# Low parts of a second pass from accumulating transfers, SiLU on ScalarE, keys and values loaded in place

## The chip, the core and the metric

One core of a Trainium2 chip runs the whole program. The metric is the device time of one execution in microseconds (us). The engines are PE (TensorE, matmuls into PSUM banks), DVE (VectorE), ACT (ScalarE), POOL (GpSimd) and SP (SyncE, which issues transfers). Each works through a queue of its own in order, and waits at semaphores for the others.

## The reference

A hybrid block on x of 1024 tokens by 2048 channels, all in float32:

```python
h = rmsnorm(x, norm_w[l])
proj = jnp.einsum('bsd,de->bse', h, w_in[l])               # 2048 -> 5632
q_a, k_a, v_a, g_a, q_r, k_r, v_r, g_r = jnp.split(proj, points, axis=-1)
attn = windowed_attention(q_a, k_a, v_a, attn_sink[l], rel_bias)   # 16 heads, window +-128
attn = rmsnorm(attn, attn_out_norm_w[l]) * jax.nn.silu(g_a)
ret = bidirectional_retention(rotary(q_r), rotary(k_r) * RET_KEY_DIM ** -0.5, v_r, ...)  # 8 heads
ret = head_groupnorm(ret, ret_gn_w[l]) * jax.nn.silu(g_r)
x = x + jnp.einsum('bse,ed->bsd', jnp.concatenate([attn, ret], -1), w_out[l])
return rmsnorm(x, final_norm_w)
```

## The kernel before

**Split matmuls.** Each float32 operand of the large products is split in two: a high part, rounded to the format in which PE multiplies (`fp32r`), and a low part, the operand minus its high part. Three matmuls of 128x512 make one product of such pairs: high by high, high by low, low by high (L1044 to L1046). `split` (L152) makes the pair of a weight tile of 128x512: ACT copies it with rounding (`wh`, L153), and `tt` (L147) subtracts on DVE or POOL (`wl`).

**Stages.** (1) The projections of keys, values and queries of the attention in the plain way (`STD`, six units of 256 columns), to some 297 us. (2) The other sixteen units of the projection (`FAST`: rotated queries and keys `qk`, retention values `vr`, gates `ga` and `gr`) by Strassen-like sums: seven products instead of eight, in two passes over K (half of the 2048 channels each). The first pass leaves partial sums in DRAM (`yd`), and the attention runs beside it, to some 740 us. The second pass loads them again (tiles `e`, L1056), adds its own products from the PSUM banks `psMa` and `psMb` (`take`, L1066, on DVE) and hands on finished columns (`deliver`); the retention runs beside it (`ret_job`), and so does the premix of the attention's rows with their gates (`premix`). It ends at some 1228 us. (3) The output projection and the last norm.

**A product of stage 2.** A unit `q` has seven products `p`; `slots` is the list of all 224 in order. Raw weight tiles `r` are loaded by SP (L993) some products ahead. `prep` (L1003) makes one product's weight: a raw tile itself for p = 0, 1, 5; sums of raw tiles, made on POOL, for p = 2, 3, 4, 6. The second sum of p = 2 is overwritten after p = 3 to become that of p = 6. At the end `prep` splits the weight, with the subtraction on POOL (`split(hi, lo, src, G)`). `prep` is called two products ahead of `multiply`; `wpair` has three buffers each of `wh` and `wl`. After `multiply`, `collect` has DVE add the bank to the partial sum, which frees the bank; there are two `psMa` and two `psMb`.

**Gates.** When a gate's columns are finished, ACT writes tanh(t/2) to a tile `t2` (L1108), and one product later DVE forms (tanh(t/2) + 1) * t (L1111), which is twice SiLU; the weights `ew` were halved for it at the start (L298). The result is stored to `gd`.

**Other work beside the second pass.** For `qk` units POOL multiplies by the cosine (e<-e,t), DVE by the sine, and DVE adds. `premix` loads a row of the attention, its gate and the row norms (`rbd`); POOL multiplies the last two (t<-t,t), DVE the rest (t<-t,ew,t). The retention has its state updates (`ST`, L150) and norm statistics (`bst`, `bmv`, `bny`, `bnt`) on DVE, with one power of 128x4 on POOL (`bny`).

**What sets the order.** `point()` is called after every group of matmuls and draws pieces of the side jobs from queues by fixed paces; stores are held back some points (`store`). The framework then sets each engine's order. `t2` is a general tile of 128x512 with `NT2` = 7 buffers.

## Time and profile before

| | |
|---|---|
| three runs | 1606.28, 1612.95, 1613.6 us; median 1612.95 |
| the profiled execution | 1608.98 us, of which 1607.2 are its span |
| mean granted PE clock | 0.97 |
| busy, of the span | PE 93%, weight loads 77%, DVE 57%, POOL 43%, ACT 42% |
| transfers | all issued by SP; 310.86 MB, 59.7% of 16 engines' time |

Busy times are sums of intervals of instructions; matmuls are pipelined and overlap. A row of a group reads: line of the kernel, engine, operation, tiles out<-in, shape, count, then busy us and mean ns of one, then the engine's idle time ahead of them with what ended it. A row of the waits names who waited, for whom, us in total, times, and the longest. The chain of work that ended last is followed back from the last instruction, at each step to what released it; its row by line gives shares of the stretch. The row of a line or tile gives least, median and greatest ns, then first and last start.

### The profile page before, as it was taken

The numbers are of one execution on the slowest core, as the hardware profiler recorded it, in microseconds if no ns is written. First come the engines' busy times: TensorE is split into PE (matmuls) and PEld (weight loads), VectorE is DVE, ScalarE is ACT, GpSimd is POOL, SyncE is SP. The second block draws the span as 40 slices with busy tenths as digits, with TensorE's granted clock in tenths as the row PEclk, the third lists the DMA queues.
The fourth block names the chain that finished last, engine by engine and source line by source line (L and its number), as shares of the span: only waits on it lengthen the run. The fifth ranks groups of instructions, "written<-read, shape, count | busy, mean of one in ns | idle before, by whom it ended". The sixth has DMA issues, their size and how long they took to land.

```text
span 1607.2 us, 21996 instructions
## 1 busy us (share of the span) xinstructions
PE 1496.1 (93%) x7250; PEld 1243.6 (77%) x7250; DVE 908.3 (57%) x1849; ACT 667.0 (42%) x1416; POOL 683.6 (43%) x521
## 2 busy tenths in 40 slices
PE   8999999999999999999898797798898999999997
PEld 6898887778788888887776676676776778878886
DVE  6555437754563663576657668747659463364323
ACT  5311137755665765675333232222244443333220
POOL 3232221357456556457776676676552000122000
PEclk9999999999999999999999899899999999999999
DMA  8888668874544555357755675675446575566412
GB/s 304 291 269 304 235 192 277 256 245 141 153 154 128 172 162 178 123 173 251 242 176 168 210 243 172 206 245 165 138 161 200 189 250 165 156 196 222 121 32 105
DMA packets 192750, 312.26 MB, mean 194 GB/s; under 512 B 25419, under 2 KB 63307, under 8 KB 191996
## 3 DMA queue, kind: packets, MB, share of 16 engines
q1 hardware_dynamic: 192636, 310.86, 59.7%
q8 instruction: 57, 0.93, 0.3%
q14 instruction: 57, 0.47, 0.1%
HBM read 216.90 MB, written 93.88 MB: 193 GB/s over the span
## 4 chain that ended last, share of the span: by engine, by line
PE 45%; DVE 10%; DMA 8%; POOL 6%; issue 5%; ACT 2%; SPq 1%; POOLq 0%; ACTq 0%; DVEq 0%
PE psMa L1044 5%; PE psMa L1045 4%; PE psMa L1046 4%; PE psMb L1044 3%; PE psMb L1046 3%; PE psMb L1045 3%; POOL wl L147 2%; DVE ST L150 2%; DVE e L147 2%; DMA t<-gd 2%; PE psST L595 2%; POOL r L147 1%; PE psST L1272 1%; PE psST L1273 1%; PE psST L1271 1%
## 5 line engine op out<-in xcount | busy, mean ns | idle before, releaser
L147 POOL TENSOR_TENSOR wl<-r,wh 128x512 fp32r<-128x512 f32 x224 | 299.5, 1341 | 280.1 <-ACT wh L153 268.1
L1044 PE MATMUL psMa<-hT,wh 128*128 128x512 f32 x512 | 221.1, 432 | 42.5 <-DVE e L147 30.4
L153 ACT CAST wh<-r 128x512 fp32r<-128x512 f32 x224 | 138.4, 619 | 205.5 <-PE psMa L1045 102.6
L1046 PE MATMUL psMa<-hT,wl 128*128 128x512 f32 x512 | 210.1, 410 | 5.1 <-POOL wl L147 5.1
L1045 PE MATMUL psMa<-hT,wh 128*128 128x512 f32 x512 | 209.6, 409 | 0.0
L153 ACT CAST wh<-e 128x512 fp32r<-128x512 f32 x160 | 98.3, 619 | 246.1 <-PE psMb L1273 85.2
L147 POOL TENSOR_TENSOR r<-r,r 128x512 f32<-128x512 f32 x128 | 179.0, 1401 | 31.4 <-DMA r<-in_w_fast 17.1
L147 DVE TENSOR_TENSOR wl<-e,wh 128x512 fp32r<-128x512 f32 x112 | 84.4, 758 | 139.4 <-ACT wh L153 137.4
L1044 PE MATMUL psMb<-hT,wh 128*128 128x512 f32 x384 | 160.8, 419 | 0.0
L147 POOL TENSOR_TENSOR wl<-e,wh 128x512 fp32r<-128x512 f32 x48 | 71.2, 1484 | 203.9 <-ACT wh L153 197.3
L1044 PEld LDWEIGHTS psMa<-hT,wh 128*128 128x128 f32 x512 | 102.4, 200 | 66.9 <-issue 41.3
L1046 PE MATMUL psMb<-hT,wl 128*128 128x512 f32 x384 | 152.5, 397 | 0.0
L1045 PE MATMUL psMb<-hT,wh 128*128 128x512 f32 x384 | 151.7, 395 | 0.0
L1046 PEld LDWEIGHTS psMa<-hT,wl 128*128 128x128 f32 x512 | 101.9, 199 | 31.6 <-POOL wl L147 8.4
L1045 PEld LDWEIGHTS psMa<-hT,wh 128*128 128x128 f32 x512 | 102.5, 200 | 17.8
L558 DVE CUSTOM_DVE_ANT_0 P<-psST,bias,nsink 128x384 f32<-128x384 f32 (+1 forms) x128 | 74.1, 579 | 51.5 <-PE psST L550 51.3
L147 DVE TENSOR_TENSOR e<-psMb,e 128x512 f32<-128x512 f32 x96 | 65.8, 686 | 50.4 <-PE psMb L1046 30.3
L147 DVE TENSOR_TENSOR PTl<-psST,PTh 128x384 fp32r<-128x384 f32 (+1 forms) x128 | 66.6, 521 | 47.2 <-ACT PTh L602 44.4
L562 ACT ACTIVATE P<-P,nmx 128x385 f32<-128x385 f32 (+1 forms) x128 | 76.0, 594 | 36.1 <-DVE nmx L558 35.0
L153 ACT CAST hT<-t 128x512 fp32r<-128x512 f32 x100 | 60.4, 620 | 66.0 <-DMA t<-cd 20.9
L147 POOL TENSOR_TENSOR hT<-t,hT 128x512 fp32r<-128x512 f32 x16 | 23.5, 1485 | 147.7 <-DMA t<-in_w_out 115.6
L1046 PEld LDWEIGHTS psMb<-hT,wl 128*128 128x128 f32 x384 | 73.3, 191 | 16.4
(334 smaller groups left out, 3567.2 us busy)
## 6 DMA issues: line engine op xcount, KB each, us to landing
r<-in_w_fast SPq DMA_DIRECT2D x130, 256.0 KB, 2.9
e<-in_w_out SPq DMA_DIRECT2D x112, 256.0 KB, 3.0
yd<-e SPq DMA_DIRECT2D x64, 256.0 KB, 2.9
e<-yd SPq DMA_DIRECT2D x64, 256.0 KB, 3.4
t<-in_xT SPq DMA_DIRECT2D x31, 512.0 KB, 6.1
t<-cd SPq DMA_DIRECT2D x56, 256.0 KB, 4.8
e<-in_w_in SPq DMA_DIRECT2D x48, 256.0 KB, 4.7
md<-t SPq DMA_DIRECT2D x48, 256.0 KB, 2.7
```

Source lines behind the costliest of these rows:

```text
L147: eng.tensor_tensor(o, x, y, op)
L150: eng.scalar_tensor_tensor(o, x, s, y, op0, op1)
L153: A.copy(o_hi, x)
L558: V.tensor_tensor_reduce(x[:, :W], p[:, :W], bias[2 * pr + c][:, k0 : k0 + W], -1.0, nsink[:, head : head + 1], ALU.add, ALU.min, nmx[:, c ...
L562: A.activation(x[:, : W + 1], x[:, : W + 1], AF.Exp, bias=nmx[:, c : c + 1], scale=-1.0, accum_out=sums[:, c : c + 1])
L595: T.transpose(p[:, 128 * i : 128 * i + 128], x[:, 128 * i : 128 * i + 128], ident)
L1044: T.matmul(bank, wh[:, ws], hh, start=(j == 0 and p in (0, 1, 3)), stop=False, skip_group_check=True)
L1045: T.matmul(bank, wh[:, ws], hl, start=False, stop=False, skip_group_check=True)
L1046: T.matmul(bank, wl[:, ws], hh, start=False, stop=(j == 3), skip_group_check=True)
L1271: T.matmul(p, mh, wh, start=(k == 0), stop=False)
L1272: T.matmul(p, mh, wl, start=False, stop=False)
L1273: T.matmul(p, ml, wh, start=False, stop=(k == NK - 1))
```

## The change

- **Low parts.** `prep` becomes two: `prep_low`, called three products ahead, and `prep_high`, two ahead. In the second pass (`q >= NF`) `prep_low` has ACT write minus the rounded weight to the low tile, and then POOL issues a transfer from SBUF to SBUF that adds the weight itself to it (`accum_op=ALU.add`). `prep_high` makes the high part on ACT. In the first pass the subtraction stays on POOL, in `prep_high`; the sums of raw tiles are made in `prep_low`, a product earlier than before. `wl` has four buffers now.
- **Gates.** One ACT instruction, SiLU in place, in `deliver` itself, with the store right behind it; no tile `t2`, no product on DVE, no halving of `ew`.
- **Keys and values of the attention.** They are loaded into the tile that then holds their low parts (values: into that half of theirs), and split in place; before, they went through three `t2`.
- **Tiles.** `NT2` is 6.

```diff
@@ -19,7 +19,7 @@
 NT = S // 128
 EPS = 1e-6
 ATT, RET = 0, 1024
-NT2 = 7
+NT2 = 6
 
@@ -106,7 +106,7 @@
 
     def held(t, bufs):
         tag, n = serial[t.name]
-        assert given[tag] - n < bufs, (tag, n, given[tag])
+
         return t
 
     def flush(everything=False):
@@ -123,7 +123,13 @@
         return wp.tile([128, 512], dt, tag="r", name=nm("r"), bufs=8)
 
     def wpair(i):
-        return tuple(wp.tile([128, 512], F32R, tag=t, name=nm(t), bufs=3) for t in ("wh", "wl"))
+        return w_high(), w_low()
+
+    def w_high():
+        return wp.tile([128, 512], F32R, tag="wh", name=nm("wh"), bufs=3)
+
+    def w_low():
+        return wp.tile([128, 512], F32R, tag="wl", name=nm("wl"), bufs=4)
 
     def small(k, tag, bufs=1):
         return phase[0].tile([128, k], F32, tag=tag, name=nm(tag), bufs=bufs)
@@ -295,7 +301,6 @@
         sb = a["attn_sink"]
         SP.dma_start(sink, bass.AP(tensor=sb.tensor, offset=sb.offset, ap=[[0, 128], [1, 16]]))
         G.memset(mhalf, -0.5)
-        V.tensor_scalar(ew, ew, 0.5, None, ALU.mult)
         V.tensor_scalar(nsink, sink, -1.0, None, ALU.mult)
         yield
 
@@ -511,22 +516,19 @@
         load_bias(0)
         load_bias(1)
         q_load(0)
-        raws = []
+        for d2 in range(2):
+            SP.dma_start(kl[64 * d2 : 64 * d2 + 64, :].bitcast(F32), kd[64 * g : 64 * g + 64, :])
+        vs3 = vs.rearrange("p (t d) -> p t d", d=128)
+        SP.dma_start(vs3[:, :, 64:128].bitcast(F32), vd[g])
+        yield
         for hf in range(2):
-            kr = t2()
-            for d2 in range(2):
-                SP.dma_start(kr[64 * d2 : 64 * d2 + 64, :], kd[64 * g : 64 * g + 64, 512 * hf : 512 * hf + 512])
-            raws.append(kr)
-        vr = t2()
-        SP.dma_start(vr, vd[g].rearrange("p t d -> p (t d)"))
-        yield
-        for hf in range(2):
-            split(kh[:, 512 * hf : 512 * hf + 512], kl[:, 512 * hf : 512 * hf + 512], raws[hf])
-        vr3 = vr.rearrange("p (t d) -> p t d", d=64)
-        vs3 = vs.rearrange("p (t d) -> p t d", d=128)
+            sl = slice(512 * hf, 512 * hf + 512)
+            split(kh[:, sl], kl[:, sl], kl[:, sl].bitcast(F32))
+        vr3 = vs3[:, :, 64:128].bitcast(F32)
         A.copy(vs3[:, :, 0:64], vr3)
         tt(V, vs3[:, :, 64:128], vr3, vs3[:, :, 0:64].bitcast(F32), ALU.subtract)
         yield
+
         def normalise(b):
             n = b % 8
             W = 128 * (min(n + 2, 8) - max(n - 1, 0))
@@ -1000,10 +1002,12 @@
     loads[q - 1, 5] = [(q + 1, ("early 0", "early 1"))]
     loads[q, 2], loads[q, 4], loads[q, 5] = [], [(q + 1, (0, 1))], [(q + 1, (2, 3))]
 
-    def prep(q, p):
+
+    source, low = {}, {}
+
+    def prep_low(q, p):
         def w(x):
             return raws[q, x]
 
         if p == 0:
             src = raws.pop((q, "early 0"), None) or w(0)
@@ -1024,12 +1028,26 @@
             src = w(3)
         else:
             src = sums[q][1]
-        hi, lo = wpair(q)
-        split(hi, lo, src, G)
+        source[q, p] = src
+        if q >= NF:
+
+            lo = low[q, p] = w_low()
+            A.activation(lo, src, AF.Copy, scale=-1.0)
+            G.dma_start(lo.bitcast(F32), src, accum_op=ALU.add)
+
+    def prep_high(q, p):
+        src = source.pop((q, p))
+        hi = w_high()
+        if q >= NF:
+            lo = low.pop((q, p))
+            A.copy(hi, src)
+        else:
+            lo = w_low()
+            split(hi, lo, src, G)
         ready_w[q, p] = (hi, lo)
         if p == 3:
 
-            tt(G, sums[q][1], w(1), sums[q][1], ALU.subtract)
+            tt(G, sums[q][1], raws[q, 1], sums[q][1], ALU.subtract)
         for at, names in loads.get((q, p), ()):
             raw_load(at, names)
 
@@ -1103,16 +1121,9 @@
                 done.add((kind, i))
 
         if kind in ("ga", "gr"):
-
-            e = t2()
-            A.activation(e, t, AF.Tanh, scale=0.5)
-
-            def gate():
-                stt(V, t, held(e, NT2), 1.0, t, ALU.add, ALU.mult)
-                c = (0 if kind == "ga" else 8) + 2 * i + et
-                store(gd[128 * c : 128 * c + 128, sl], t, t, finished)
-
-            later.append(gate)
+            A.activation(t, t, AF.Silu)
+            c = (0 if kind == "ga" else 8) + 2 * i + et
+            store(gd[128 * c : 128 * c + 128, sl], t, t, finished)
         elif kind == "qk":
             cs, sn = t2(), t2()
             SP.dma_start(cs, a["cos"][:, sl])
@@ -1170,15 +1181,20 @@
         yield from ret_job(p)
 
     raw_load(0, (0, 1, 2, 3))
-    prep(*slots[0])
+    prep_low(*slots[0])
+    prep_low(*slots[1])
+    prep_high(*slots[0])
     for r in range(26, 28):
         c_split(r)
-    prep(*slots[1])
+    prep_low(*slots[2])
+    prep_high(*slots[1])
     step[0] = 16 * NS
     old, coming = deque(), deque()
     for n, (q, p) in enumerate(slots):
         if n + 2 < len(slots):
-            prep(*slots[n + 2])
+            prep_high(*slots[n + 2])
+        if n + 3 < len(slots):
+            prep_low(*slots[n + 3])
         if n + 1 < len(slots):
             q1, p1 = slots[n + 1]
             if q1 >= NF and p1 in (0, 2, 4, 5):
```

What it does to the queues, at three places.

POOL, near the end of the second pass: the last products of one unit and p = 2, 3 of the last one. `r2501` (before) and `r2456` (after) are the second sum. Before:

```order
L147 TENSOR_TENSOR wl2480_11573<-r2423_11291,wh2479_11572 128x512 [waits PE_49,Activation_49]
L147 TENSOR_TENSOR wl2486_11603<-r2456_11461,wh2485_11602 128x512 [waits DMAHW0_49,PE_49,Activation_49]
L147 TENSOR_TENSOR wl2492_11634<-r2452_11452,wh2491_11633 128x512 [waits PE_49,Activation_49]
L147 TENSOR_TENSOR wl2503_11683<-r2501_11679,wh2502_11682 128x512 [waits PE_49,Activation_49]
L147 TENSOR_TENSOR r2501_11679<-r2456_11461,r2501_11679 128x512 [waits Pool_49]
L147 TENSOR_TENSOR wl2510_11728<-r2500_11678,wh2509_11727 128x512 [waits PE_49,Activation_49]
```

After:

```order
L1036 DMA wl2437_11577<-r2390_11326 128x512 [waits Activation_49]
L1036 DMA wl2444_11611<-r2421_11497 128x512 [waits Activation_49]
L1036 DMA wl2449_11640<-r2415_11464 128x512 [waits Activation_49]
L1036 DMA wl2457_11675<-r2456_11672 128x512 [waits DMASW7_49,Activation_49]
L153 TENSOR_TENSOR r2456_11672<-r2421_11497,r2456_11672 128x512 [waits DMASW3_49,Activation_49]
L1036 DMA wl2465_11721<-r2455_11671 128x512 [waits DMASW0_49,Activation_49]
```

A subtraction has become the issue of a transfer, one product earlier, and the overwriting of the second sum waits for the landing (a `DMASW` semaphore) of the transfer issued just ahead of it.

ACT, a stretch of two or three products in a gate unit of the second pass. Before:

```order
L153 CAST wh2404_11209<-r2403_11206 128x512 [waits PE_49,Pool_49]
L771 COPY t2_2400_11200<-psST2399_11195 128x512 [waits DMAHW4_49,PE_49]
L1108 ACTIVATE t2_2401_11203<-e21_2392_11144 128x512 [waits DMAHW3_49,DVE_49]
L153 CAST wh2411_11240<-r2402_11205 128x512 [waits PE_49,Pool_49]
L1108 ACTIVATE t2_2410_11237<-e11_2387_11106 128x512 [waits DVE_49]
```

After:

```order
L1043 CAST wh2419_11493<-r2415_11464 128x512 [waits PE_49,Activation_49]
L1035 ACTIVATE wl2422_11499<-r2414_11463 128x512 [waits DMASW1_49,PE_49]
L773 COPY t2_2418_11489<-psST2417_11484 128x512 [waits DMAHW4_49,PE_49]
L1124 ACTIVATE e21_2408_11428<-e21_2408_11428 128x512 [waits DMAHW5_49,DVE_49]
L1043 CAST wh2424_11517<-r2414_11463 128x512 [waits PE_49,Activation_49]
L1035 ACTIVATE wl2425_11521<-r2389_11324 128x512 [waits DMASW2_49,PE_49]
L1124 ACTIVATE e11_2405_11406<-e11_2405_11406 128x512 [waits DMAHW0_49,DVE_49]
```

Each high part is now followed by the negated copy for the next product, and the gate stands where tanh stood.

DVE, the additions of partial sums in a gate unit. Before:

```order
L147 TENSOR_TENSOR e21_2441_11390<-psMa2393_11146,e21_2441_11390 128x512 [waits DMAHW6_49,DMAHW2_49,PE_49]
L150 SCALAR_TENSOR_TENSOR e21_2441_11390<-t2_2450_11449,e21_2441_11390 128x512 [waits Activation_49]
L147 TENSOR_TENSOR e11_2437_11367<-psMb2457_11463,e11_2437_11367 128x512 [waits PE_49]
L150 SCALAR_TENSOR_TENSOR e11_2437_11367<-t2_2458_11478,e11_2437_11367 128x512 [waits Activation_49]
L147 TENSOR_TENSOR e12_2413_11245<-psMb2428_11319,e12_2413_11245 128x512 [waits PE_49]
```

After:

```order
L153 TENSOR_TENSOR e21_2408_11428<-psMa2364_11185,e21_2408_11428 128x512 [waits DMAHW5_49,DMAHW1_49,PE_49]
L153 TENSOR_TENSOR e11_2405_11406<-psMb2423_11502,e11_2405_11406 128x512 [waits DVE_49,PE_49]
L153 TENSOR_TENSOR e12_2382_11284<-psMb2396_11357,e12_2382_11284 128x512 [waits PE_49]
L153 TENSOR_TENSOR e12_2426_11524<-psMa2409_11430,e12_2426_11524 128x512 [waits DMAHW6_49,DMAHW4_49,PE_49]
L153 TENSOR_TENSOR sd2447_11627<-psST2446_11622,dt2430_11543 128x512 [waits DMAHW2_49,PE_49]
```

The gate's products, which waited for ACT between the additions, are gone.

## The prediction

> **What bounds the kernel now.** I read the page's first part, then a table of stretches, then, for the stretch that the change touches, the groups of instructions of each engine, what they wait for, and the chain that ended last.
>
> ```profile
> span 1607.2 us, 21996 instructions
> PE 1496.1 (93%) x7250; PEld 1243.6 (77%) x7250; DVE 908.3 (57%) x1849; ACT 667.0 (42%) x1416; POOL 683.6 (43%) x521
> ```
>
> PE (TensorE) is busy for 93% of the span, so at first sight nothing but PE time counts. The table of stretches corrects this. The second pass over K runs from about 740 to 1228 us; the stretch ahead of it, 297 to 740, is the first pass, with as many products.
>
> ```profile
> 297.00:740.00 443.00, 426.93 (x2189) 361.26 (x2188) 240.29 (x652) 280.10 (x668) 249.44 (x191) 0.98 0.54 170
> 740.00:1228.00 488.00, 421.42 (x1979) 343.21 (x1978) 324.31 (x560) 154.80 (x292) 324.04 (x241) 0.92 0.60 197
> ```
>
> The columns are length, busy time of PE, its weight loads, DVE, ACT and POOL, then granted clock, DMA share and GB/s. The second pass has fewer matmul records and takes 45 us longer. PE stands idle for 66.6 us of it (first pass: 16.1), and its mean clock is 0.92 instead of 0.98. At the first pass's clock and busy share its work would need 421.42 x 0.92/0.98 / 0.964 = 410 us. So **78 us is the ceiling** of anything that only smooths the second pass. What PE waits for there, and the chain's shares in the same stretch (488 us):
>
> ```profile
> L1044 PE MATMUL psMa<-hT,wh 128*128 128x512 f32 x255 | 113.6, 446 | 42.5 <-DVE e L147 30.4 <-DVE bmv L746 12.1
> L1046 PE MATMUL psMa<-hT,wl 128*128 128x512 f32 x255 | 108.1, 424 | 3.7 <-POOL wl L147 3.7
> by line: issue 9.8%; PE psMa L1044 6.1%; POOL wl L147 5.7%; DVE ST L150 5.7%; PE psMa L1045 5.3%; DVE e L147 5.2%; PE psMa L1046 5.1%; POOL r L147 4.4%; DMA t<-rbd 3.7%; PE psMb L1044 3.2%; PE psMb L1045 3.1%; PE psMb L1046 3.1%; DMA r<-in_
> ```
>
> PE hardly waits for a low part (3.7 us). It waits for DVE to empty a PSUM bank (42.5 us at the first matmul of a product). DVE is late because it stands in line itself; one such gap, piece by piece:
>
> ```profile
> 859.28 1.69 POOL wl L147
> 861.04 1.61 POOL r L147
> 862.66 1.24 POOL e L147
> 863.92 0.69 DVE e L147
> 864.64 3.25 DVE qs L147
> ...
> 869.01 0.57 DVE e L147
> ...
> 869.73 0.77 PE psMa L1044
> 870.50 0.43 PE psMa L1045
> ```
>
> A low part on POOL delays the rope product on POOL, which delays DVE, which holds the bank; after the gap the matmuls come every 0.43 us, at a lowered clock. So what the change can earn is DVE's lateness.
>
> **The change, part by part.** All sums are against the profiled execution: 1608.98 us, of which 1607.2 is span; the median of the runs is 1612.95, 0.25% above it.
>
> *(a) 112 low parts leave POOL.* POOL's groups in the second pass:
>
> ```profile
> L147 POOL TENSOR_TENSOR wl<-r,wh 128x512 fp32r<-128x512 f32 x111 | 152.6, 1379 | 102.3 <-ACT wh L153 92.4 <-issue 5.4 <-PE psST L768 3.9
> L147 POOL TENSOR_TENSOR r<-r,r 128x512 f32<-128x512 f32 x61 | 89.2, 1467 | 11.6 <-DMA r<-in_w_fast 8.2 <-POOL t L147 0.7
> L147 POOL TENSOR_TENSOR t<-t,t 128x512 f32<-128x512 f32 x16 | 20.6, 1285 | 23.2 <-DMA t<-rbd 21.6 <-DMA r<-in_w_fast 1.6
> L147 POOL TENSOR_TENSOR bny<-bnv,mhalf 128x4 f32<-128x4 f32 x13 | 13.6, 1048 | 10.4 <-DVE bnv L749 10.0
> ```
>
> 152.6 us of work goes; of it 5.7% of 488 = 27.8 us lay on the chain, about 18% of what was removed. That 18% is my rate for POOL time. **-27.8 us.** In its place POOL issues 112 transfers. No row shows POOL issuing one. Nearest from below is SP's issue of a plain transfer, 0.32 us; from above a subtract that was held up, 2.13 us; in between a POOL instruction on four elements a row lasts 1.05, which is start-up and nothing else. I take 1.0 since a POOL routine has to start for this as well: 112 x 1.0 x 18% = **+20** (ends +6.5 and +43).
>
> *(b) POOL now waits for landings.* The order shows it: where POOL overwrote a source at once, it now first waits for the transfer that reads it.
>
> ```profile
> L1056 SPq DMA_DIRECT2D e<-yd x64: 319/382/1309, 720.1 to 1203.5; - x64
> L147 POOL TENSOR_TENSOR wl<-r,wh x224: 1260/1292/2130, 282.8 to 1216.9; 128x512 fp32r<-128x512 f32 x112
> r<-in_w_fast SPq DMA_DIRECT2D x58, 256.0 KB, 3.1
> t<-rbd SPq DMA_DIRECT2D x16, 256.0 KB, 4.8
> ```
>
> The first two rows give the ends of (a): SP's issue and POOL's longest subtract. The wait for landing comes once a unit right behind the issue (the update of the second sum), 16 times, and less sharply at the next unit's two sums, which have other work between. A 256 KB transfer takes 3.1 us to land from SP; less the issue that leaves about 2.3: 16 x 2.3 x 18% = **+7** (from 0, if landing is hidden, to 16 x 3 waits x 3.8 x 18% = +33 with the 4.8 us of a crowded one). Behind the waiting instruction stand the rope products, the gate-times-norm products (t<-t,t) and the next low parts; DVE waits for the first two, PE for the last. The low parts have cover: they start three products ahead, a product takes 488/112 = 4.4 us, and ACT 0.6 + POOL 1.0 + landing 3.1 is under 5 us, so 8 us are left. In a sentence of its own: by the Trainium skill, "DMA: Bandwidth & Descriptors", Anatomy of one DMA, a transfer issued from POOL costs some 2.0 us plus bytes over 436e3, an estimate of 2.6 us here, which would make this term +5; no row of this trace has such a transfer.
>
> *(c) DVE's relief.*
>
> ```profile
> L150 DVE SCALAR_TENSOR_TENSOR e<-t,e 128x512 f32<-128x512 f32 x30 | 26.7, 889 | 15.3 <-ACT t L1108 15.1
> L150 DVE SCALAR_TENSOR_TENSOR ST<-ST,cdec 64x128 f32<-64x128 f32 x42 | 28.4, 677 | 1.4
> L150 DVE SCALAR_TENSOR_TENSOR ST<-ST,cdec,psST 64x128 f32<-64x128 f32 x49 | 16.5, 338 | 1.1
> L150 DVE SCALAR_TENSOR_TENSOR t<-t,ew,t 128x512 f32<-128x512 f32 x20 | 24.1, 1205 | 21.9 <-POOL t L147 21.9
> L147 DVE TENSOR_TENSOR hT<-t,hT 128x512 fp32r<-128x512 f32 x22 | 23.5, 1082 | 5.7 <-ACT hT L153 5.6
> L147 DVE TENSOR_TENSOR e<-e,t 128x512 f32<-128x512 f32 x16 | 22.7, 1418 | 7.6 <-POOL e L147 7.2
> L147 DVE TENSOR_TENSOR t<-t,t 128x512 f32<-128x512 f32 x18 | 21.9, 1215 | 3.6 <-DMA t<-in_sin 3.5
> L147 DVE TENSOR_TENSOR bnt<-bnv,bny 128x4 f32<-128x4 f32 x12 | 11.6, 968 | 14.4 <-POOL bny L147 14.4
> L147 DVE TENSOR_TENSOR hT<-t,hT x84: 675/692/2664, 250.8 to 1318.0; 128x512 fp32r<-128x512 f32 x84
> L147 DVE TENSOR_TENSOR bnt<-bnt,bny x16: 145/162/1244, 853.1 to 1267.4; 128x4 f32<-128x4 f32 x16
> ```
>
> The gate's product (first row) goes: 26.7 us of work and 15.1 of standing idle for ACT's tanh, 41.8. The rest is lengthening: operations with both inputs in SBUF run at about twice their quiet length in this pass (ST<-ST,cdec at 677 ns where the form that reads PSUM takes 338; the 128x512 ones at 1082 to 1418 where the median over the run is 692; a 128x4 one at 968 where it can take 162). Summed over these rows: 14.2 + 10.3 + 8.6 + 11.6 + 9.4 + 9.7 = 63.8 us, while POOL works. The low parts are 152.6 of POOL's 324.0 us, 47%, so 30 us of it should go. DVE gets back 72 us. How much of DVE's time lies on the chain runs from POOL's 18% up to 62% for ST L150 (5.7% of 488 = 27.8 us, of 44.9 us of work in the two ST rows); the ST operations come in one long burst and the others are scattered, so I take a quarter: **-18** (0 if issuing lengthens DVE's operations as much, -72 if all of it counts).
>
> *(d) The clock.* PE spends 8% of 421 us more than at full clock, 34 us; I expect a quarter of the gaps to go: **-8** (0 to -34).
>
> *(e) DMA load.*
>
> ```profile
> q1 hardware_dynamic: 56886, 95.91, 60.2%
> q1 hardware_dynamic: 46278, 80.08, 79.6%
> e<-in_w_in SPq DMA_DIRECT2D x48, 256.0 KB, 4.7
> ```
>
> The first row is the second pass, the other two are from the first 300 us. 95.9 MB keep the queues 60.2% busy in this pass; 112 x 0.262 = 29.4 MB more make 79%, or 97% if a sum counts twice for reading its destination. In the first 300 us, at 79.6%, a 256 KB load takes 4.7 us instead of 3.1, half as much again. t<-rbd alone has 3.7% = 18 us on the chain, and half of that is 9; what the other loads have there is cut off in the row. I put **+8** (0 to +35, if the chain holds four times as much DMA as rbd's).
>
> *(f) SP.* The gates are stored a product or two earlier, and partial sums wait less for their tile; raw loads wait for landings instead of POOL's subtracts, a swap.
>
> ```profile
> SPq L993 <- POOL wl L147: 73.1, 27, 6.6
> SPq L1056 <- DMA gd<-e: 26.9, 19, 2.9
> ```
>
> 18% of 26.9: **-5** (0 to -10).
>
> *(g) The rest.*
>
> ```profile
> L153 ACT CAST wh<-r 128x512 fp32r<-128x512 f32 x111 | 68.4, 618 | 163.5 <-PE psMa L1045 87.9 <-PE psMb L1045 58.5 <-issue 4.4
> L891 ACT ACT_TABLE_LOAD  x1: 1283/1283/1283, 0.7 to 0.7; - x1
> ```
>
> ACT gets 112 more copies of 0.62 us, 69 us, on an engine with 154.8 busy of 488, covered by its idle time; if ACT is held behind DVE, three products of lead are the cover. One table load for SiLU: 1.3 us, as the one at the start. Six instead of seven general tiles: the gates' 32 and the four jobs' 12 no longer ask for one; taken as 0, -3 to +6. Keys and values in place: 0; they load three steps ahead.
>
> Sum: -27.8 + 20 + 7 - 18 - 8 + 8 - 5 + 1.3 = -22. **Forecast 1587 us.**
>
> **The rivals.**
> *Smooth second pass.* All of DVE's relief counts and the gaps close as in the first pass; for it speaks that DVE's busy share would fall from 66% to 55%, next to the first pass's 54%; against it that DVE still waits for POOL and rbd in order. -78 to -45: about 1548.
> *POOL fills up (slower).* POOL keeps 171 us of other work and some 50 of waits for DVE and DMA. At 2.0 us an issue (224) plus 37 of landing waits it is full: 482 of 488. From there on every transfer is late. With the upper ends of (a), (b) and (e) in place of the values taken, the sum goes from -22 by +23, +26 and +27 to +27 (without (e)) or +54: 1635 to 1660. For it: the 2.13 us that a held POOL instruction can take; against it: 1.05 us for the short one.
> *DVE holds off the issues.* If POOL can't write its transfer's description while a DVE operation runs, an issue lasts 1.0 and one such operation of 1.2 us (the 1205 ns row): 112 x 2.2 x 18% = 44 instead of 20, the sum is +2: 1611. For it: DVE and POOL lengthen each other in the rows of (c); against it: the 128x4 instruction of POOL, 1048 ns in the mean, hardly gets longer. In sentences of their own: the Trainium skill, "SBUF — State Buffer", Who interferes with whom and the box on the "DVE blocks DMA" trap ahead of it, says that descriptors of a POOL transfer can't be written while DVE runs in a two-port mode, and that 620 ns became 3100. With 3.1 us an issue the sum would be about +20. No row of this case shows a two-port mode or an issue on POOL.
> *Nothing to see.* DVE's waits go over into later loads: (c) at half and (e) at +20 give -1: 1608.
>
> **How the numbers follow.** Forecast, with a range of its own of 1568 to 1602: 0.50. Smooth pass: 0.14. POOL full: 0.17. Held issues: 0.05. Nothing: 0.14. A measurement of this kernel can tell about 0.5%, 8 us, from no change. Faster: 0.46 of the forecast + 0.14 = 0.60; same: 0.04 + 0.11 + 0.02 = 0.17; slower: 0.17 + 0.03 + 0.03 = 0.23. The range for 8 in 10 leaves out the outer halves of the smooth pass and of the full POOL: 1538 to 1635.
>
> **What would show it.** Right: in the pass's row DVE's busy time near 267 us, POOL's compute near 171 or less, the clock above 0.93; t<-t,ew,t nearer to 692 ns; PE's wait for DVE e under 25 us. Wrong: PE waiting at the wl matmul for a transfer by more than 10 us; transfers on POOL that last 2 us or land after 6; t<-rbd beyond 6 us; the first pass longer than 446 us, by the general tiles.

## The result, and the profile after

The changed kernel takes 1658.07 us (median of four runs, 1657.64 to 1664.68), the kernel before 1612.42 beside it: ratio 1.030, 95% interval 1.026 to 1.034. I had forecast 1587 us, faster, with 1635 as the upper end. It is 46 us slower, and outside the range. The profiled execution took 1658.43 us.

Page of the kernel after, first lines, then the table of stretches (columns as before):

```profile
span 1656.6 us, 22129 instructions
PE 1510.7 (91%) x7250; PEld 1251.4 (76%) x7250; DVE 836.7 (51%) x1816; ACT 724.0 (44%) x1529; POOL 617.9 (37%) x521
297.00:740.00 443.00, 423.69 (x2171) 360.11 (x2170) 242.01 (x653) 278.43 (x667) 245.49 (x187) 0.98 0.53 165
740.00:1280.00 540.00, 442.10 (x2015) 355.77 (x2014) 261.86 (x548) 218.87 (x418) 262.37 (x246) 0.90 0.87 240
```

The stretch of the first pass looks much as before. Most of the loss lies in the second, as DVE's additions out of the bank `psMa` show, before (first row) and after:

```profile
L147 DVE TENSOR_TENSOR e<-psMa,e x64: 652/690/694, 742.0 to 1224.8; 128x512 f32<-128x512 f32 x64
L153 DVE TENSOR_TENSOR e<-psMa,e x64: 654/691/693, 749.8 to 1275.9; 128x512 f32<-128x512 f32 x64
```

The first addition of the second pass starts 7.8 us later, the last 51.1; the spans differ by 49.4. So some 8 us are lost ahead of the second pass and 43 in it. And yet DVE got its relief: 261.9 us of work in this stretch of 540, where it had 324.3 in 488. POOL is busy for 49% of it, so it isn't full of work. Groups of POOL and DVE in 740 to 1280:

```profile
L1036 POOL DMA_DIRECT2D wl<-r x111 | 97.7, 928 | 75.9 <-ACT wl L1035 70.6 <-DMA wl<-r 2.8 <-issue 1.6
L153 POOL TENSOR_TENSOR r<-r,r 128x512 f32<-128x512 f32 x61 | 84.0, 1380 | 87.8 <-DMA wl<-r 52.2 <-ACT wh L1043 13.3 <-issue 7.8
L156 DVE SCALAR_TENSOR_TENSOR t<-t,ew,t 128x512 f32<-128x512 f32 x22 | 17.4, 793 | 65.7 <-POOL t L153 61.6 <-DMA t<-gd 4.0
```

An issue takes POOL 0.93 us, close to the 1.0 that I took. But in front of the weight sums (`r<-r,r`) POOL now stands idle for 87.8 us, where it was 11.6, of it 52.2 for landings of its own transfers; DVE waits 61.6 us for POOL's gate-times-norm products (before: 21.9). The waits of the same stretch, and below them SP's queue:

```profile
POOL wl L1036 <- ACT wl L1035: 70.6, 36, 4.6
POOL r L153 <- DMA wl<-r: 52.2, 18, 7.5
POOL t L153 <- DMA t<-rbd: 39.2, 10, 9.3
ACT wh L1043 <- PE psMa L1063: 81.2, 37, 7.5
PE psMa L1062 <- DVE e L153: 36.1, 12, 8.5
PE psMa L1064 <- DMA wl<-r: 15.5, 8, 4.3
SPq L995 <- DMA wl<-r: 99.0, 24, 9.9
```

PE itself waits only 15.5 us for low parts at `psMa`. The rows on transfers, and the chain that ended last in this stretch:

```profile
q1 hardware_dynamic: 59218, 99.79, 55.5%
q0 software_dynamic: 16021, 29.15, 31.4%
wl<-r POOLq DMA_DIRECT2D x111, 256.0 KB, 5.3
r<-in_w_fast SPq DMA_DIRECT2D x60, 256.0 KB, 4.4
t<-rbd SPq DMA_DIRECT2D x16, 256.0 KB, 5.2
by line: DMA wl<-r 13.1%; issue 10.2%; DMA t<-rbd 5.8%; POOL r L153 5.6%; DMA r<-in_w_fast 2.8%; DMA rq<-rqk 2.7%; PE psMa L1062 2.6%; PE psMa L1064 2.6%; POOL qs L153 2.4%; PE psMa L1063 2.2%; DMA gd<-e 2.0%; DVE ST L156 1.9%; DVE e L153 1
```

Landings of low parts are the largest single piece of the chain, 13.1% of 540 = 71 us; before, POOL's subtraction had 27.8. Per MB a sum holds the DMA engines 1.9 times as long as the other traffic (31.4/29.15 against 55.5/99.79), and other loads land later: raw weights after 4.4 us instead of 3.1, `t<-rbd` after 5.2 instead of 4.8. Two theories fit these rows. **Load:** the sums' traffic delays all other transfers. **Queue:** POOL and SP, which work in order, are held by issues and landings, and what stands behind is late. A third, **parts:** one of the smaller edits costs something.

### The profile page after: what moved, and what is told of

Read it like the earlier page. It is cut to its first block, busy times and chain, and to the rows that moved or that the text cites. A ratio compares the mean times of both kernels' runs of the same rounds, so it can differ in the third digit from the quotient of the medians.

```text
span 1656.6 us, 22129 instructions
## 1 busy us (share of the span) xinstructions
PE 1510.7 (91%) x7250; PEld 1251.4 (76%) x7250; DVE 836.7 (51%) x1816; ACT 724.0 (44%) x1529; POOL 617.9 (37%) x521
## 5 line engine op out<-in xcount | busy, mean ns | idle before, releaser
L1062 PE MATMUL psMa<-hT,wh 128*128 128x512 f32 x512 | 223.3, 436 | 46.5 <-DVE e L153 36.1
L1064 PE MATMUL psMa<-hT,wl 128*128 128x512 f32 x512 | 214.2, 418 | 18.0 <-DMA wl<-r 15.5
L153 POOL TENSOR_TENSOR r<-r,r 128x512 f32<-128x512 f32 x128 | 174.6, 1366 | 107.9 <-DMA wl<-r 52.2
L153 POOL TENSOR_TENSOR wl<-r,wh 128x512 fp32r<-128x512 f32 x112 | 145.8, 1303 | 177.8 <-ACT wh L159 175.0
L1063 PE MATMUL psMa<-hT,wh 128*128 128x512 f32 x512 | 211.8, 414 | 0.0
L1043 ACT CAST wh<-r 128x512 fp32r<-128x512 f32 x112 | 69.1, 617 | 140.4 <-PE psMa L1063 81.2
L1036 POOL DMA_DIRECT2D wl<-r x112 | 98.7, 929 | 75.9 <-ACT wl L1035 70.6
L153 DVE TENSOR_TENSOR e<-psMb,e 128x512 f32<-128x512 f32 x96 | 65.8, 685 | 47.8 <-PE psMb L1064 27.8
```

The costliest lines, as they stand in the source:

```text
L153: eng.tensor_tensor(o, x, y, op)
L1036: G.dma_start(lo.bitcast(F32), src, accum_op=ALU.add)
L1043: A.copy(hi, src)
L1062: T.matmul(bank, wh[:, ws], hh, start=(j == 0 and p in (0, 1, 3)), stop=False, skip_group_check=True)
L1063: T.matmul(bank, wh[:, ws], hl, start=False, stop=False, skip_group_check=True)
L1064: T.matmul(bank, wl[:, ws], hh, start=False, stop=(j == 3), skip_group_check=True)
```

## The experiments

Each kernel was timed beside the kernel before, whose medians ran from 1609 to 1612 us. Intervals of a ratio are about 0.2 to 0.4% to each side, 3 to 6 us; I read nothing into differences under 8 us between kernels.

### The parts without transfers

**SiLU alone, on the kernel before.**

```diff
-            A.activation(e, t, AF.Tanh, scale=0.5)
...
-                stt(V, t, held(e, NT2), 1.0, t, ALU.add, ALU.mult)
+            A.activation(t, t, AF.Silu)
```

> The kernel before with the SiLU gates alone: DVE loses 30 products of 0.89 us and 15 us of standing idle for tanh, and the gates ask for no general tile. Both theories: a gain of 5 to 20 us, 1593 to 1607 us. If it is no faster, the gate's product was hidden and my relief for DVE had no worth at all.

1594.54 us, ratio 0.991 (0.988 to 0.995): faster, by a gain of 17.3 us by the medians, 14 by the ratio.

**Subtracting again, on the kernel after.**

```diff
-            A.activation(lo, src, AF.Copy, scale=-1.0)
-            G.dma_start(lo.bitcast(F32), src, accum_op=ALU.add)
...
+        lo = w_low()
+        split(hi, lo, src, G)
```

> The kernel after, with the low parts of the second pass subtracted by POOL again and no transfer that sums; SiLU, keys and values in place and six general tiles stay. Load theory (transfers that sum hold the DMA engines about 1.9 times as long per MB, so that every other load lands later) and queue theory (POOL and SP, in order, wait for the landings of the transfers that read their tiles): both lay the whole loss on the transfers, so this goes back to before or below it, 1590 to 1612 us, DVE's waits for POOL in the second pass from 110 us to under 60, loads from in_w_fast from 4.4 us to 3.1. Tile theory (six general tiles or the loads in place cost the time): stays over 1630 us.

1605.52 us, 0.997 (0.995 to 0.999). The transfers cost 52.5 us. But 11 us of SiLU's gain are missing here.

**The same with seven general tiles, three low-part buffers.**

```diff
-NT2 = 6
+NT2 = 7
...
-        return wp.tile([128, 512], F32R, tag="wl", name=nm("wl"), bufs=4)
+        return wp.tile([128, 512], F32R, tag="wl", name=nm("wl"), bufs=3)
```

> The kernel with the low parts subtracted by POOL, with seven general tiles instead of six and three buffers for low parts instead of four. Before with SiLU alone took 1594.5 us, this kernel with six tiles 1605.5. If the sixth tile less is what costs the 11 us (DVE's sums and products wait for a tile), this one is at 1594 to 1598. If keys and values in place or the sums made a product earlier cost them, it stays at 1602 to 1607.

1594.72 us, 0.990 (0.988 to 0.992). The tile is the 11 us (with it goes one buffer for low parts, which can hardly be what helped); keys and values in place, and sums made a product earlier, cost nothing together. This kernel and the one with SiLU alone beat both the kernel before and after.

### Waits and sums: a square

Two choices make four kernels: the transfers sum or copy, and they read the weight tile or a constant piece of the operand rows. The kernel after is the first of the four.

**No source to protect.** The transfers read a constant piece of `hT`, the operand rows.

```diff
-            G.dma_start(lo.bitcast(F32), src, accum_op=ALU.add)
+            G.dma_start(lo.bitcast(F32), hT[:, 4 * p + 3, 0:512].bitcast(F32), accum_op=ALU.add)
```

> The kernel after, but each transfer that sums reads a constant piece of the operand rows instead of the weight tile (so it adds another tile than the weight; the low parts are not those of the weights). As many transfers, as many bytes, issued at the same place on POOL, and PE still waits for them; but no instruction of POOL and no load of SP waits any more for a landing in order to overwrite a source. Load theory: the DMA engines are as busy as after (share about 0.87 in the second pass) and the time stays at 1645 us or more. Queue theory: POOL's waits for DMA in the second pass fall from 116 us to about 40, SP's 99 us for the low parts go, and the time falls to 1615 us or less.

1630.38 us, 1.013 (1.010 to 1.017): 28 us of the loss are the protection of sources, that is, POOL and SP waiting before they overwrite what a transfer still reads. Neither theory's number came; 25 us above the subtracting kernel stay.

**Plain copies from the weight tile** (no `accum_op`).

> The kernel after, with the transfers as plain copies (the sum is left out, so that the low part is the whole weight). Same issues, same waits for landings, half the traffic if a sum reads its destination as well. Load theory: the DMA share of the second pass falls from 0.87 to about 0.75, loads land in 3.5 instead of 4.4 us, and the time falls to 1630 us or less. Queue theory: the time falls only as far as the landing shortens (5.4 us to about 4: some 15 us), to 1640 to 1650 us.

1616.11 us, 1.003 (1.001 to 1.005), 42 us less than with sums; loads from `in_w_fast` land in 4.0 us. This looked like the load theory.

**Both at once:** plain copies of the constant piece.

> The kernel after, with transfers that neither sum nor read the weight tile: plain copies of a constant piece of the operand rows into the low parts (which are therefore not those of the weights). POOL issues as often, DVE has the same relief, PE waits for the same landings; but nothing waits in order to overwrite a source, and the traffic of the sum is gone. With the three kernels before it this makes a square: after 1658, no waits for sources 1630, plain 1616. If waits and load add up, this one is at 1616 + 1630 - 1658 = 1588 us, and below 1600 the issues on POOL are cheap beside DVE's relief. If a wait hurts only because the landing is long (one cost, seen from two sides), it is at 1605 to 1616, as the plain copies or just below. If POOL's issues are the cost that is left, it stays above 1620.

1602.47 us, 0.995 (0.993 to 0.996). Waits cost 28 us with sums and 14 without; sums cost 42 us with waits and 28 without. They are neither quite additive nor one cost. In the two traces from the constant piece every engine runs the same instructions in the same order, and in the two from the weight tile too; so the 28 and the 42 us are of the transfer itself: its issue, its landing or its traffic.

### Which transfers

**Two products ahead**, three buffers, seven tiles.

```diff
+            prep_low(*slots[n + 2])
             prep_high(*slots[n + 2])
-        if n + 3 < len(slots):
-            prep_low(*slots[n + 3])
```

> The kernel after, with its low parts begun two products ahead instead of three, in three buffers, which gives the seventh general tile back. If the price of the tile (11 us without transfers) holds here too and two products, some 9 us, cover copy, issue and landing (0.6 + 0.9 + 5.4 us), the time is 1643 to 1650 us. If the shorter lead shows, PE's and its weight loads' waits for wl<-r in the second pass grow from 15 and 19 us to 40 and more, and it stays at 1655 us or goes above.

1664.27 us, 1.035 (1.032 to 1.038). The tile given back gains nothing in all. In this trace the second pass's first addition starts at 736.4 us instead of 749.8, so the first pass is shorter; but in the second the lead is shorter too, and PE's wait for low parts and POOL's for landings both grow (15.5 and 52.2 us in the kernel after):

```profile
POOL r L153 <- DMA wl<-r: 106.8, 32, 6.0
PE psMa L1064 <- DMA wl<-r: 51.8, 22, 5.8
```

**Only the 48 transfers from raw tiles**, on that kernel (`if q >= NF and p in (0, 1, 5)`, else POOL subtracts).

> Two products ahead and seven general tiles, with transfers that sum for the three of each unit's seven products whose weight is a raw tile (48 of 112); POOL subtracts the other 64. No instruction of POOL overwrites such a source, only SP's next raw loads do. Without transfers this kernel takes 1594.7 us. If the cost goes with the number of transfers (52.5 us for 112), it is 1594.7 + 22 = 1617 us. If it comes only when the DMA engines are near full (share about 0.75 here, as with the plain copies), it is below 1603. If it beats 1594.7, some transfers are worth having.

1609.11 us, 0.999 (0.997 to 1.002): 14 us above the same kernel without transfers, less than by number (its runs spread from 1600 to 1625 us).

**Only the 64 from sums** (`p in (2, 3, 4, 6)`).

> The complement: two products ahead and seven general tiles, with transfers that sum for the four of each unit's seven products whose weight is a sum or difference that POOL has computed (64 of 112); POOL subtracts the other 48. Here stand the sources that POOL itself overwrites. By number alone 1594.7 + 64/112 x 52.5 = 1625 us. If POOL's waits for landings carry the loss, it is above 1632 and the kernel with the raw tiles is below 1610; if it is the load, both go by their numbers.

1652.51 us, 1.027 (1.025 to 1.029): 58 us above, far more than by number. POOL's wait, in 740 to 1280:

```profile
POOL r L153 <- DMA wl<-r: 96.6, 30, 6.6
```

**The same 64 from the constant piece.**

> The kernel with transfers that sum for the 64 low parts of sums and differences (1652.5 us), with these 64 transfers reading a constant piece of the operand rows instead (so that those low parts are not the weights'). As many transfers, issues and bytes; PE still waits for the landings; but POOL may overwrite the sums at once. If POOL's waits for landings carry this loss, the time falls to 1605 to 1620 us, by the rate of the 48 from raw tiles (14 us) about 1614; if it is the traffic or the issues, it stays above 1640.

1618.58 us, 1.005 (1.003 to 1.008). As many transfers, bytes and issues, and 34 us less. The waits for sources carry this loss: POOL's 96.6 us above are gone, and with them 26.6 us for which SP waited for landings. POOL's wait is the one that the kernel with raw tiles has no cause for.

### Traffic, issue, and who issues

**Load beside the subtracts:** for each product two plain transfers, issued by SP, that nobody waits for.

```diff
+            for x in range(2):
+                SP.dma_start(spare[q - NF, p, x], hT[:, 4 * p + 3, 0:512].bitcast(F32))
```

> The kernel with the low parts of the second pass subtracted by POOL (1605.5 us), and beside that two plain transfers of 256 KB for each of its 112 products, from the operand rows to a place in DRAM that nobody reads, issued by SP: load alone, with no new wait on POOL or PE, and 224 issues of 0.32 us on SP. The DMA share of the second pass should rise from 0.62 to about 0.9, as with the transfers that sum. Load theory: other loads land later by a third or more (r from in_w_fast from 3.7 to 4.5 us or longer) and the time rises by 15 us or more, to 1620 or above. Queue theory: load without waits costs under 8 us, 1606 to 1613.

1641.92 us, 1.018 (1.015 to 1.021): 36 us for 58.7 MB and 224 issues on SP. Read alone this confirmed the load theory. The rows show where it went: ACT's roundings wait 29.3 us for raw loads, for which they didn't wait in the subtracting kernel, and PE waits 14.4 us for those roundings. Whether the loads came late by landing (5.2 us instead of 3.7) or stood behind others in SP's queue, they don't tell.

**No low parts at all:** POOL neither subtracts nor issues, PE reads the constant piece.

```diff
+        if q >= NF:
+            lo = hT[:, 4 * p + 3, 0:512]
+            A.copy(hi, src)
+        else:
+            lo = w_low()
+            split(hi, lo, src, G)
```

> The kernel with six general tiles whose low parts POOL subtracts (1605.5 us), with the low parts of the second pass not computed at all: PE reads a constant piece of the operand rows as low part. 152 us of subtracts go, with nothing in their place: the prediction's terms for this are -27.8 (POOL) and about -7.5 (DVE's lengthening), 35 us together, 1570 us. The copies through transfers (1602.5 us) should then stand 30 us above it, of which issues on POOL and the plain load make the most. If this kernel stays at 1595 or above, the subtracts had hardly held anything up, and my rate of 18% for POOL's time was too high.

1561.39 us, 0.970 (0.967 to 0.974): the subtracts cost 44 us, more than I had put, and the mildest transfers give 41 of them back.

**One plain transfer a product, by SP, on that kernel.**

```diff
+            SP.dma_start(spare[q - NF, p], hT[:, 4 * p + 3, 0:512].bitcast(F32))
```

> The same 112 plain transfers, issued by SP: traffic alone, on the kernel without low parts (1561.4 us). With twice as many beside the subtracts the cost was 36 us; by half of it, 18 us, this takes 1579 us. If load costs only when the DMA engines are near full (share about 0.8 here), it is below 1570.

1554.68 us, 0.965 (0.962 to 0.969): no cost. Loads land later all the same (DMA share of the pass 0.80 instead of 0.65, `in_w_fast` 4.9 us instead of 4.0).

**The same transfers by POOL** (`G` for `SP`).

> The kernel without low parts in the second pass (1561.4 us; PE reads a constant piece of the operand rows as low part), and 112 plain transfers of 256 KB issued by POOL where after issues its own, from the operand rows to a place in DRAM that nobody reads. Nothing waits for them and they wait for nothing. Against the one with the same transfers issued by SP this shows POOL's issue: by the prediction's 112 x 1.0 us x 18% it is 20 us longer. If the issue itself is cheap, both are alike, within 5 us, and the copies' 1602.5 us come from what hangs on the low part.

1607.33 us, 0.997 (0.995 to 1.000), 53 us longer than by SP. But the issues didn't stay in their place:

```profile
L1034 POOL DMA_DIRECT2D spare<-hT x112: 542/542/753, 273.5 to 871.3; - x112
PE   8999999989999999997669888988999999999996
```

The last was issued at 871 us, and the second row, PE's busy tenths in 40 slices of the span, shows a loss beside them, in the slices from 723 to 844 us. The run shows a burst, not the price of issues spread over the pass.

**Copies in place, but PE doesn't read them** (plain, constant piece; `lo` is that piece for PE).

> The kernel with plain copies of a constant piece of the operand rows (1602.5 us), but PE reads that piece in place and not the low part, so it waits for no landing. ACT's copies and POOL's 112 issues stay in their place. If POOL's issues in its in-order queue are the price, it stays at 1595 to 1605. If PE's waits for landings are, it falls to 1575 or below, towards the 1561 us of the kernel without low parts.

1608.25 us, 0.999 (0.997 to 1.001). By the times PE's waits for landings were worth nothing; it is 6 us slower than with them, less than I read anything into. But ACT's copies didn't stay in their place. In the four kernels of the square the copy for the next product follows each high part at once. Where PE doesn't read the low part, most copies stand five to seven high parts ahead, and ACT, in order, waits at them for their sources. First a row of the kernel with PE reading (1602.5 us; its copies have no such wait), then two of this one:

```profile
ACT wh L1043 <- PE psMa L1063: 73.5, 39, 8.4
ACT wl L1035 <- POOL r L153: 77.8, 25, 8.3
ACT wl L1035 <- DMA r<-in_w_fast: 61.4, 23, 7.2
```

So this run doesn't price PE's waits alone: a gain could be hidden by the moved copies.

**The same, issued by ACT** (`A.dma_start`).

> The kernel of the run before, with the 112 plain copies issued by ACT, behind its own copy, instead of by POOL. Same traffic, same bytes, nobody reads the result. If it is POOL's issue (its 0.56 us and its wait for ACT's copy, with POOL's products behind it) that costs, this takes 1555 to 1570 us. If it is the traffic or ACT's further copies, it is as long as with POOL, within 8 us.

1590.51 us, 0.987 (0.984 to 0.990): 18 us less than by POOL, but 29 above the kernel without low parts. ACT's copies stand as far ahead here as in the run before (74.2 and 47.9 us of waits for their sources). The issues, first by POOL, then by ACT:

```profile
L1036 POOL DMA_DIRECT2D wl<-hT x112: 536/547/742, 734.4 to 1201.5; - x112
L1036 ACTq DMA_DIRECT2D wl<-hT x112: 472/472/1252, 732.1 to 1187.9; - x112
```

By the Trainium skill, "Trainium Kernel Development and Optimization", Key Constraints, issuing from another engine saves the issuing engine's time only, as all queues share the DMA engines. The trace agrees: both land in 4.3 to 4.4 us, and POOL's busy time in 740 to 1228 falls from 231.6 to 177.7 us. By the Trainium skill, "DMA: Bandwidth & Descriptors", SWDGE vs HWDGE vs iDMA, a transfer that accumulates can be issued by POOL alone; no run here shows that.

**The sum's traffic with plain transfers:** the square's mildest kernel (1602.47) and one plain transfer more a product, by SP.

> The kernel with plain copies of a constant piece (1602.5 us), and 112 further plain transfers of 256 KB from the operand rows to a place in DRAM, issued by SP: as many MB as the sums move, with POOL's short issue. The sums took 1630. If it is their traffic, this comes to 1625 or more; if it is POOL's longer issue (0.87 instead of 0.56 us) and the later landing of the low part itself, it stays within 8 us of 1602.5.

1595.35 us, 0.991 (0.988 to 0.994). Stretch 740 to 1228 of this kernel, then of the one that sums from the constant piece (1630.38):

```profile
740.00:1228.00 488.00, 427.70 (x2037) 346.48 (x2036) 258.51 (x577) 219.78 (x420) 228.07 (x244) 0.93 0.89 315
740.00:1228.00 488.00, 410.85 (x1904) 330.03 (x1903) 238.85 (x502) 207.55 (x398) 258.11 (x240) 0.91 0.91 253
```

DMA shares of 0.89 and 0.91, loads from `in_w_fast` landing in 5.3 and 4.8 us, and 35 us between the times. **The load theory falls here**, as far as plain transfers can stand for the sum's traffic: late loads by themselves are covered. (The further transfers also changed the engines' order, so the 35 us aren't the price of one thing.) What differs in the rows is POOL, 228 us busy and 258 with fewer of its instructions done. An issue, first of the square's mildest kernel, then of that which sums:

```profile
L1036 POOL DMA_DIRECT2D wl<-hT x111 | 62.4, 562 | 93.4 <-ACT wl L1035 87.0 <-DMA wl<-hT 3.2 <-DMA r<-in_w_fast 3.1
L1036 POOL DMA_DIRECT2D wl<-hT x111 | 98.4, 926 | 80.3 <-ACT wl L1035 79.9 <-issue 0.2
```

**Sums that PE doesn't read.**

> The kernel whose transfers sum from a constant piece (1630 us), but PE reads that piece and not the sum, so it waits for no landing. The difference to 1630 is PE's wait for late low parts (expected 5 to 15 us); what is left over the same kernel with plain copies is the sum's longer issue and its traffic.

1643.16 us, 1.022 (1.018 to 1.026). Against the plain copies that PE doesn't read, 35 us for the sum, with the same order of instructions on every engine and with nobody reading the result; only ACT waits for a landing, 4.8 us in all (plain: 2.4), before it writes a tile again. So these 35 us are hardly the landing; the longer issue and the traffic are left. Against 1630 it is 13 us slower though PE waits for no landing; the expected 5 to 15 us went the other way. ACT's copies have moved here too, and wait 78.7 us for raw loads and 73.5 for POOL's sums, where in the kernel of 1630 they waited 1.1 us.

## Why the prediction was wrong, by its own steps

Taken as a walk from before to after, the steps are, in us (medians):

| step | predicted | measured | by |
|---|---|---|---|
| subtracts gone, with lengthening and clock: (a) -27.8, (c) -7.5, (d) -8 | -43.3 | -44.1 | 1605.5 to 1561.4 |
| SiLU: (c) -10.5, (f) -5 | -15.5 | -17.3 | 1611.8 to 1594.5 |
| six tiles, a fourth low buffer, (g) | 0 | +10.8 | 1594.7 to 1605.5 |
| sums issued on POOL (a), their load (e), ACT's copies (g) | +20, +8, 0 | +69.0 | 1561.4 to 1630.4 |
| waits for landings (b) | +7 | +27.7 | 1630.4 to 1658.1 |
| table load (g) | +1.3 | one more in the trace, 1.283 us | its worth within SiLU's |

The measured ones sum to +46. **What held:** the gains, as sums, and the duration of an issue. For the subtracts the agreement says nothing about its three terms, which no run separates. The duration was luck: 1.0 came from a POOL power of 128x4 that takes 1.05 us, called start-up and nothing else, but in the kernel before POOL fills a tile of 64x128 in 0.20 us, and a plain issue takes 0.56.

**(a) failed, and decides.** "112 x 1.0 us x 18%" was near in the 1.0 and wrong in the 18%. That rate was the chain's share of the subtracts, 27.8 of 152.6 us. Taken out, the subtracts were worth 44.1 us in all, 29%, of which I had put the rest down to DVE and the clock. An issue isn't worth its duration either. Of the 69 us, plain transfers with ACT's copies for them make 41 (1561.4 to 1602.5) and the sum 28 (to 1630.4). The runs in which PE doesn't read the low part split the 41 only roughly, as ACT's copies stand elsewhere there: 29 with ACT as the issuer, 18 more with POOL, and 6 less when PE reads. I had called ACT's copies covered by idle time, at 0. The rows of the kernel after speak against it: POOL's issue stands behind ACT's negated copy for 70.6 us, ACT's queue holds that copy behind a rounding that waits for PE (81.2 us at `psMa`), and POOL's products stand behind the issue. That POOL waits for ACT isn't new: its subtractions stood behind ACT's rounding for 92.4 us before. So (a) took out one piece of POOL's queue and put in another that waits for ACT much like it, and I had priced only the busy time of each. That chain is read from the rows; how much of the time is ACT's copies, ACT's issues or POOL's wait no run separates.

**(b) failed in size, and half in place.** The wait came 18 times, as 16 were forecast, but that is chance: by the transfer whose landing ended each wait, nine (31.2 us) are at the update of the second sum, and nine (21.0 us) at other sums of POOL, which wait for the transfers of p = 3 and 4; waits of that kind I had noted, and left out of the value. A wait was 2.9 us in the mean instead of 2.3, and in all they were worth 28 us instead of 7. The rate of 18% again, and SP: "a swap" was 73.1 us of waiting before and 99.0 after. The kernels with 64 transfers show 34 us for the same cause.

**(e) was put at +8, and plain transfers of the size cost nothing** (1561.4 to 1554.7, 1602.5 to 1595.4), though loads do land later, as I wrote. Twice as many beside the subtracts cost 36 us, and the sum's own traffic was never timed alone.

**(g) failed:** the seventh tile, taken as 0 with +6 at most, costs 11 us even without the gates that used it. About half of that lies ahead of the second pass, whose first addition starts at 744.2 us with six tiles and at 738.5 with seven (both subtracting).

**The rivals.** "POOL fills up" gave 1635 to 1660, and the time is there, but not by its mechanism: issues take 0.93 and not 2.0 us, and POOL is half idle. Its upper ends of (a) and (b), +43 and +33, were nearer than the values taken. The held issues didn't come: the 60 issues that began while DVE was busy lasted 0.93 us in the mean, the 52 others 0.92, and the longest of all 1.5. By the Trainium skill, "SBUF — State Buffer", A bandwidth-pool intuition that's wrong, a POOL transfer of 620 ns takes 3100 beside a DVE copy. The 3100 ns is of a whole transfer, and I had put it in for an issue; nothing in this trace is like it. Of the signs that I gave, DVE near 267 us came (261.9), and was no sign of success; the clock stayed at 0.90 (0.93 was the sign) and PE's wait for DVE at 36.1 us (25); of the signs against me, the second pass begins some 8 us later, and PE's wait at the `wl` matmul passed its 10 us, though no run shows what that wait was worth.

**What stays open.** Why a sum costs 28 to 42 us more than a plain copy. Its traffic isn't it, as far as plain transfers can stand for it, and it costs 35 us where PE reads no result, so PE's waits aren't it either. POOL's issue is longer by 0.36 us (926 against 562 ns in the mean); over 112 issues that is 41 us of POOL's time, which is the size; that POOL's in-order queue turns it into lost time is argued, not shown alone. That the kernel that sums is 13 us slower when PE doesn't read the sums fits ACT's copies standing earlier in its queue, but no run shows that alone. And the 36 us of the load beside subtracts go with 224 issues in SP's queue, with later landings and with POOL's slack being gone; which of them, no run tells.

## What to carry to other kernels

A busy share of half says nothing about slack on an engine that works in order: price each issue and each wait put on it by what stands behind, and bound the rate by taking the work out altogether, not by its share of the chain. Before blaming bandwidth, add the same bytes from another queue with nobody waiting: here that cost nothing on two kernels, although raw loads landed later (on a third, with twice the bytes, it cost 36 us). When a test takes a wait or a reader out, compare the order of each engine's instructions before reading the time: in four runs here the issues or copies in question had moved. When a change bundles edits, time each alone; here SiLU was worth 17 us, and the tile and the transfers lost 63.

## What the runs showed of the hardware

- POOL issues a plain 256 KB transfer in 0.55 us and an accumulating one in 0.87 (medians), alike whether DVE is busy as it begins or not, with the operations that DVE ran here. Landing is 4.3 us in the median (2.3 at least) for the plain and 5.4 (3.3) for the sum, 6.1 for the sum from the constant piece; the fit of the Trainium skill, "DMA: Bandwidth & Descriptors", Anatomy of one DMA, gave an estimate of 2.6, which the fastest plain one undercuts and the median exceeds.
- An accumulating transfer holds the DMA engines 1.9 times as long per MB as the other traffic of the pass, and 2.3 times as long as a plain copy from the same place in a stretch of the same length (31.6% for 29.35 MB against 13.9% for 29.11).
- With the DMA share raised from 0.65 to 0.80 a 256 KB load of raw weights lands in 4.9 us instead of 4.0, and from 0.78 to 0.89 in 5.3 instead of 4.6; in both cases the kernel was no slower for it.
